# A decoder step on one core: Strassen weight forms made eight K tiles at a time, and 16 K tiles instead of 14 in the heads

## The chip, the cores and the metric

The kernel runs on one core of one Trainium2 chip. The metric is the device time of one execution in microseconds (us); the median of three runs is given. TensorE multiplies, ScalarE (ACT in the profile) and VectorE (DVE) work element by element, GpSimd (POOL) and SyncE (SP) mostly start transfers.

## The reference, cut to what matters

Two layers are computed for 512 prompt tokens and 8 sample tokens, which share all weights. The model width is 2048; everything is float32.

```python
def trunk_layer(x, p_i, pos, conv_buf, ret_S, norm_g, w_in, conv_w, gn_g, w_out, w_pg, w_ple):
    h = rmsnorm(x, norm_g)
    z = h @ w_in                                   # 2048 -> 8192 columns
    b_c, c_c, x_c, g_c, q, k, v, g_r = split_projection(z)
    conv_y, new_buf = short_conv(c_c * x_c, conv_buf, conv_w)
    y_conv = b_c * conv_y * jax.nn.silu(g_c)
    q = rope(q...); k = rope(k...) * (RET_HEAD_DIM ** -0.5)
    o, new_S = retention(q, k, v, ret_S, retention_log_gamma())
    ...                                            # norm over each head
    y_ret = (o * gn_g) * jax.nn.silu(g_r)
    x = x + jnp.concatenate([y_conv, y_ret], axis=-1) @ w_out      # 2048 -> 2048
    x = x + jax.nn.sigmoid(x @ w_pg) * (p_i @ w_ple)               # 2048 -> 2048
    return x, new_buf, new_S
```

A final RMS norm follows. Four large products per layer (w_in, w_out, w_pg, and the small w_ple) hold nearly all the arithmetic.

## The kernel before

**Layout.** Activations lie transposed: 16 K tiles of 128 model columns, each 128 partitions by 520 tokens (512 and 8). The tokens are cut into two halves, LEFT and RIGHT, of 260. A weight column block is 128 columns wide, so a matmul is a 128x128 weight tile times 260 tokens.

**Three matmuls for one.** To keep float32 accuracy each operand is split into a rounded part and a remainder. `split_w` makes the two weight parts: ScalarE copies the raw weights into `hi` (L229), VectorE subtracts to get `lo` (L230). `mm3` then issues `hi*x_hi`, `hi*x_lo` and `lo*x_hi` (lines L247, L248, L249).

**Pairs by Strassen.** Two column blocks are computed together by `pair`. Where its number of rows `s` is not 0, the first `s` K tiles go through `strassen` in the seven-product form: column blocks, even and odd K tiles and token halves form a 2x2 by 2x2 product. Each of the seven products runs over q = s/2 K tiles. `raws` loads the four raw weight forms w11, w21, w22 and w12, `add` combines them in place on VectorE (L319, four times per pair), and `times` splits a form and multiplies it. The K tiles from `s` to 16 are done plainly afterwards. With s = 16 there is nothing left over: the pair then takes three PSUM banks (a, b, d) instead of four, and two of the results go straight into slots.

**Banks and copies.** A bank is copied out while products keep being added to it: for instance bank `a` takes w11·k1, is copied into d, takes w21·t2 (the third product), is copied into z0, takes w11·t3 (the fifth), is read out again, and takes w22·t4. Those copies are line L307, on ScalarE (`copy`) or VectorE (`plus`). The next matmul on the bank waits for its copy.

**Chunks.** `add` and `times` cut the q tiles into chunks of at most CHA and CHS tiles. With 4, seven tiles are cut 3 and 4, eight tiles 4 and 4. `CHL` cuts the loads. Raw forms live in a ring of 32 tiles taken in eights (so four forms), the split parts in a ring of 60 tiles.

**Stages.** For each layer: the heads (16 pairs of w_in for q, k, v and the gate of four retention heads; the first two of layer 0 are done outside `pair`), the convolution (16 pairs of w_in), the mixer output (8 pairs of w_out) and the gate (8 pairs of w_pg, 7 in the last layer). `HEADS`, `CONVS`, `OUT_ROWS` and `GATES` hold `s` for each pair. Retention itself (`steps`), sample states and operand sums are spread between them.

**Order.** The program is written once and a list scheduler, with priorities, decides the order of the instructions on each engine. Every engine then works through its own list in that order; an instruction that waits holds back all behind it on its engine.

Of the kernel before, what the change touches and what calls it, by code (L numbers as in the profile page):

```python
# [28 lines left out]
EPS = 1e-6  # L29
NSLOT = 75  # L30
CH = 4
CHS = 4
CHA = 4
CHL = 4
CK = 256
BUSY = 10**9
# [13 lines left out]
EARLY = 6  # L50


HEADS = [[0, 0, 0, 8] + [14] * 12, [0] + [14] * 15]
CONVS = [[14] * 2 + [16] * 13 + [14]] * 2
OUT_ROWS = [[0, 8, 16, 16, 16, 16, 16, 0]] * 2

MIXED, MIX = 64, [*range(8, 14), *range(8), 14, 15]
# [134 lines left out]
def trunk_kernel(  # L192
# [32 lines left out]
    def split_w(raw, slot=False):  # L225
        n = raw.shape[1]
        hi, lo = (getr()[:, :n] if slot and not split_ring.fits(n // P) else split_ring.get(n // P) for _ in range(2))
        with tc.high_priority(offset=WPRIO):
            S.activation(hi, raw, AF.Copy)  # L229
            V.tensor_tensor(lo, raw, F(hi), SUB)  # L230
        return hi, lo

    def chunks(a, b, most=CH):

        n = (b - a + most - 1) // most
        e = [a + (b - a) * i // n for i in range(n + 1)] if n else [a]
        return list(zip(e, e[1:]))
# [52 lines left out]
    def strassen(x, src0, src1, s, step=None):  # L290
# [24 lines left out]
        def add(out, x, y, op):  # L315
            for i, j in chunks(0, q, CHA):
                n = slice(P * i, P * j)
                with tc.high_priority(offset=WPRIO):
                    V.tensor_tensor(out[:, n], x[:, n], y[:, n], op)  # L319

        def times(out, raw, xs, start, more):
            for i, j in chunks(0, q, CHS):
                w = split_w(raw[:, P * i : P * j])
                product(out, w, 0, xs[i:j], start and i == 0, j == q, more)
                split_ring.put(*w)
# [237 lines left out]
    def norm_g(l, k):  # L563
        return vec[:, 16 * l + k : 16 * l + k + 1]
# [97 lines left out]
    def from_dram(src):  # L662
        def load(k):
            t = get()
            SIDE.dma_start(t, src[k])
            return t

        return load

    xs = []  # L670
    X = Operands(HEADS[0][2:] + CONVS[0], from_dram(xT), gain=lambda k: norm_g(0, k))
    X.todo = [t for t in ((i, False, True) for i in range(max(X.rows) // 2))]
# [43 lines left out]
    for l in range(DEPTH):  # L716
# [456 lines left out]
        if not tail:  # L1173
            X = Operands(HEADS[l + 1] + CONVS[l + 1], next_in, RESERVE_NEXT, gain=lambda k, l=l: norm_g(l + 1, k))
        for m in range(0, KT - tail, 2):
# [303 lines left out]
```

## Time and profile before

| what | value |
|---|---|
| median of three runs (lowest, highest) | 2166.96 us (2166.78, 2170.64) |
| span of the profiled execution | 2167.3 us |
| TensorE (PE) busy | 2147.8 us, 99% |
| VectorE (DVE) busy | 1896.1 us, 87% |
| ScalarE (ACT) busy | 1264.5 us, 58% |
| mean traffic of the transfers | 179 GB/s |

The page gives no other time for the profiled execution than its span, 2167.3 us, which is 0.3 us above the median. The profile gives busy time per engine, groups of equal instructions with their mean length, who waited for whom, and every instruction in order of time. A matmul's listed length (some 0.28 us) is longer than the distance between two matmuls (some 0.12 us), since they overlap in the array; a gap between two matmuls is therefore read from their starts.

By the lines that appear in the trace the heads of layer 0 run to about 505 us, the convolution to about 705 us, the mixer output to about 870 us, the gate to about 1110 us; those of layer 1 end at about 1530, 1785, 1930 and 2110 us.

### The profile page before, as it was taken

How to read it: one execution, taken by the hardware profiler on the slowest of the kernel's cores; microseconds unless marked ns; L12 is line 12 of the kernel's file. 1: busy time of each engine (PE TensorE's matmuls, PEld its weight loads, DVE VectorE, ACT ScalarE, POOL GpSimd, SP SyncE). 2: the span in 40 equal slices, each digit the busy share in tenths (PEclk: the TensorE clock that was granted, in tenths of full speed). 3: DMA queues.
4: the chain of work that ended last, by engine and by line, in shares of the span. 5: the costliest groups of instructions: out<-in, count | busy, mean ns of one | idle time of the engine just before them, and what ended most of it. 6: DMA issues, size and time to landing. Idle time of an engine off the chain costs nothing. (4 is left out here: it accounts for less than half of the span.)

```text
span 2167.3 us, 48178 instructions
## 1 busy us (share of the span) xinstructions
PE 2147.8 (99%) x17861; PEld 2142.1 (99%) x17861; DVE 1896.1 (87%) x3849; ACT 1264.5 (58%) x2647; POOL 430.6 (20%) x746
## 2 busy tenths in 40 slices
PE   9999999999999999999999999999999999999998
PEld 9999999999999999999999999999999999999998
DVE  8889988998999987987997988989999998879884
ACT  8656655565555655655765655565645555456565
POOL 2313222211001211200212222231111022011011
PEclk9999999999999999999999999999999999999999
DMA  8555565545543745645645566664464355566455
GB/s 288 171 175 197 181 217 184 178 157 175 158 129 118 238 156 187 215 154 160 215 144 175 172 213 191 189 209 170 151 182 149 120 158 202 176 207 200 128 164 198
DMA packets 182861, 387.31 MB, mean 179 GB/s; under 512 B 25888, under 2 KB 56352, under 8 KB 182624
## 3 DMA queue, kind: packets, MB, share of 16 engines
q1 hardware_dynamic: 128704, 212.98, 31.6%
q0 software_dynamic: 53056, 169.84, 23.8%
q8 instruction: 140, 2.29, 0.4%
q10 hardware_dynamic: 864, 1.39, 0.2%
q14 instruction: 97, 0.79, 0.1%
HBM read 318.96 MB, written 65.15 MB: 177 GB/s over the span
## 5 line engine op out<-in xcount | busy, mean ns | idle before, releaser
L247 PE MATMUL ps_g<-slot,split 128*128 128x260 f32 x5465 | 1531.6, 284 | 7.2 <-ACT slot L307 2.9
L248 PE MATMUL ps_g<-slot,split 128*128 128x260 f32 x5465 | 1534.3, 282 | 0.3 <-DVE slot L555 0.3
L249 PE MATMUL ps_g<-slot,split 128*128 128x260 f32 x5461 | 1519.9, 283 | 0.5 <-DVE split L230 0.5
L229 ACT ACTIVATE split<-raw 128x512 fp32r<-128x512 f32 (+2 forms) x1347 | 777.3, 596 | 583.1 <-DVE raw L319 213.2
L247 PEld LDWEIGHTS ps_g<-slot,split 128*128 128x128 f32 x5465 | 1024.0, 188 | 10.1 <-ACT slot L307 3.7
L248 PEld LDWEIGHTS ps_g<-slot,split 128*128 128x128 f32 x5465 | 1028.5, 188 | 0.5 <-DVE slot L555 0.5
L249 PEld LDWEIGHTS ps_g<-slot,split 128*128 128x128 f32 x5461 | 1019.8, 188 | 1.0 <-DVE split L230 1.0
L230 DVE TENSOR_TENSOR split<-raw,split 128x512 fp32r<-128x512 f32 (+2 forms) x1346 | 849.2, 652 | 172.5 <-PE ps_g L248 85.4
L319 DVE TENSOR_TENSOR raw<-raw 128x512 f32<-128x512 f32 (+1 forms) x660 | 428.9, 660 | 32.5 <-DMA raw<-wi 23.7
L307 ACT ACTIVATE slot<-ps_g 128x260 f32<-128x260 f32 x336 | 127.4, 381 | 140.6 <-PE ps_g L249 122.7
L551 ACT ACTIVATE slot<-slot 128x520 fp32r<-128x520 f32 (+1 forms) x212 | 109.2, 562 | 46.6 <-DVE slot L414 11.1
L552 DVE TENSOR_TENSOR slot<-slot,slot 128x520 fp32r<-128x520 f32 (+1 forms) x212 | 124.4, 620 | 4.1 <-ACT slot L551 3.9
L781 POOL DMA_DIRECT2D o_rets<-slot x64 | 35.3, 552 | 351.6 <-DVE slot L780 131.7
L307 DVE TENSOR_TENSOR slot<-ps_g,slot 128x260 f32<-128x260 f32 x168 | 70.9, 424 | 6.0 <-PE ps_g L249 3.7
L869 POOL DMA_DIRECT2D slot<-hs x64 | 46.2, 724 | 118.7 <-DVE split L230 42.7
L814 POOL DMA_DIRECT2D hs<-slot x64 | 35.6, 556 | 139.3 <-DVE slot L755 61.3
L780 DVE SCALAR_TENSOR_TENSOR slot<-slot,vs,slot 128x256 f32<-128x256 f32 x128 | 56.1, 481 | 4.5 <-ACT slot L776 4.3
L746 DVE TENSOR_TENSOR slot<-slot,slot 128x520 f32<-128x520 f32 x80 | 55.8, 698 | 4.7 <-DMA o_rets<-slot 3.7
L770 POOL DMA_DIRECT2D slot<-sret x64 | 35.5, 554 | 114.6 <-ACT split L229 37.3
L1058 POOL DMA_DIRECT2D slot<-x1s x76 | 40.8, 538 | 87.6 <-PE ps_g L249 27.2
L1209 POOL DMA_DIRECT2D x2s<-slot x30 | 16.4, 545 | 201.6 <-DVE slot L1204 200.6
L771 POOL DMA_DIRECT2D slot<-kq x64 | 34.9, 547 | 106.0 <-DVE slot L876 22.2
(217 smaller groups left out, 1733.8 us busy)
## 6 DMA issues: line engine op xcount, KB each, us to landing
raw<-wi SPq DMA_DIRECT2D x377, 256.0 KB, 3.9
raw<-wo SPq DMA_DIRECT2D x128, 256.0 KB, 5.4
raw<-wg SPq DMA_DIRECT2D x122, 256.0 KB, 4.1
raw<-wi SPq DMA_DIRECT2D x136, 192.0 KB, 4.0
slot<-x1s POOLq DMA_DIRECT2D x76, 260.0 KB, 5.1
slot<-sret POOLq DMA_DIRECT2D x64, 256.0 KB, 4.0
hs<-slot POOLq DMA_DIRECT2D x64, 256.0 KB, 4.0
slot<-hs POOLq DMA_DIRECT2D x64, 256.0 KB, 5.2
```

The lines of the kernel that those rows point to most:

```text
L229: S.activation(hi, raw, AF.Copy)
L230: V.tensor_tensor(lo, raw, F(hi), SUB)
L247: PE.matmul(out, wh, xh, start=start, stop=False, skip_group_check=more)
L248: PE.matmul(out, wh, xl, start=False, stop=False, skip_group_check=more)
L249: PE.matmul(out, wl, xh, start=False, stop=stop, skip_group_check=more)
L307: fn(*args)
L319: V.tensor_tensor(out[:, n], x[:, n], y[:, n], op)
L551: keep(S.activation(hi, src[:, n], AF.Copy))
L552: V.tensor_tensor(lo, src[:, n], F(hi), SUB)
L746: V.tensor_tensor(out[:, n], v, table[:, n], MUL)
L780: keep(V.scalar_tensor_tensor(st[:, c], k, vs[:, h, e, b : b + 1], st[:, c], MUL, ADD))
L869: SIDE.dma_start(t[:, :512].rearrange("p (m n) -> p m n", m=2), src)
```

## The change

Two constants and two tables. `CHS` and `CHA` go from 4 to 8, so that `times` splits a whole form with one ScalarE and one VectorE instruction, and `add` combines whole forms with one VectorE instruction. The head pairs with 14 rows now have 16; of the convolution pairs the first two of each layer go from 14 to 16, and only the last one keeps 14.

```diff
-CHS = 4
-CHA = 4
+CHS = 8
+CHA = 8
...
-HEADS = [[0, 0, 0, 8] + [14] * 12, [0] + [14] * 15]
-CONVS = [[14] * 2 + [16] * 13 + [14]] * 2
+HEADS = [[0, 0, 0, 8] + [16] * 12, [0] + [16] * 15]
+CONVS = [[16] * 15 + [14]] * 2
```

So 27 head pairs and 4 convolution pairs go from 14 rows to 16. All 84 Strassen pairs are touched by the chunks, except those with 8 rows (three of them), whose four tiles were one chunk already. The counts of instructions change as follows (name, shape: before, now):

| engine, line, shape | before | now |
|---|---|---|
| PE, all matmuls | 17827 | 17734 |
| DVE, all | 3851 | 2898 |
| ACT, all | 2655 | 1995 |
| SP, loads | 886 | 824 |
| DVE L230 `lo`, 128x1024 / x896 / x768 / x512 / x384 / x256 | 0 / 0 / 0 / 1031 / 249 / 66 | 546 / 14 / 7 / 143 / 4 / 4 |
| ACT L229 `hi`, the same shapes | 0 / 0 / 0 / 1032 / 249 / 66 | 546 / 14 / 7 / 143 / 4 / 4 |
| DVE L319 `add`, the same shapes | 0 / 0 / 0 / 520 / 140 / 0 | 312 / 8 / 4 / 12 / 0 / 0 |
| ACT L307 copies from bank to bank | 121 | 90 |

**What the order becomes on TensorE.** The place is a convolution pair of layer 0. A bank's name carries a number, so that equal numbers are the same bank in the same pair; `[waits ...]` names the engine whose semaphore is waited for. Before, bank `a` of the pair is ps_g_7737. Its third product ends here:

```order
L247 MATMUL ps_g_7737<-slot27_152_1588,split_73 128x260
L248 MATMUL ps_g_7737<-slot28_153_1589,split_73 128x260
L249 MATMUL ps_g_7737<-slot27_152_1588,split_73 128x260
L247 MATMUL ps_g_7977<-slot2_3_119,split_73 128x260 [waits Activation_49]
L248 MATMUL ps_g_7977<-slot2_3_119,split_73 128x260
L249 MATMUL ps_g_7738<-slot7_8_168,split_73 128x260 [waits DVE_49]
```

Of the 24 rows that follow, 12 belong to bank b and 12 to the next pair's first product (ps_g_7977). Then the fifth product of the same bank begins, which waits for the copy:

```order
L247 MATMUL ps_g_7977<-slot21_22_332,split_73 128x260
L248 MATMUL ps_g_7977<-slot21_22_332,split_73 128x260
L249 MATMUL ps_g_7977<-slot21_22_332,split_73 128x260
L247 MATMUL ps_g_7737<-slot52_79_777,split_73 128x260 [waits Activation_49]
L248 MATMUL ps_g_7737<-slot53_80_778,split_73 128x260
```

Now, at the same place, bank `a` is ps_g_7205 and bank b ps_g_7206. The end of the third product and the start of the fifth on TensorE:

```order
L247 MATMUL ps_g_7205<-slot30_143_1407,split_73 128x260
L248 MATMUL ps_g_7205<-slot34_144_1408,split_73 128x260
L249 MATMUL ps_g_7205<-slot30_143_1407,split_73 128x260
L247 MATMUL ps_g_7206<-slot7_8_168,split_73 128x260 [waits Activation_49]
L248 MATMUL ps_g_7206<-slot8_9_169,split_73 128x260
L247 MATMUL ps_g_7205<-slot52_79_777,split_73 128x260 [waits Activation_49]
L248 MATMUL ps_g_7205<-slot53_80_778,split_73 128x260
```

The half of bank b's product and the beginning of the next pair, which filled the place, have moved behind: two matmuls are left between the bank's last one and its next one, where 24 were. Counted over the whole program, a matmul that waits for a ScalarE copy (L307) of its own bank stands this many rows behind that bank's last matmul:

| rows behind | 1 | 3 | 4 | 5 | 7 | 8 to 16 | 17 or more |
|---|---|---|---|---|---|---|---|
| before, waits | 0 | 0 | 0 | 1 | 1 | 6 | all others |
| now, waits | 6 | 39 | 3 | 1 | 3 | 12 | all others |

**What it becomes on ScalarE.** The place is the same pair. Before, around the copies of bank a (ps_g_7737):

```order
L307 ACTIVATE slot10_426_7740<-ps_g_7739 128x260 [waits DMASW4_49,PE_49]
L229 ACTIVATE split_73<-raw_72 128x512 [waits DVE_49]
L307 ACTIVATE slot10_426_7740<-ps_g_7737 128x260 [waits PE_49]
L229 ACTIVATE split_73<-raw_72 128x512 [waits DMAHW5_49]
L229 ACTIVATE split_73<-raw_72 128x512 [waits DMAHW4_49]
```

Now (ps_g_7205 is bank a, ps_g_7207 bank d):

```order
L307 ACTIVATE slot49_426_7208<-ps_g_7207 128x260 [waits DMASW4_49,PE_49]
L229 ACTIVATE split_73<-raw_72 128x1024 [waits DVE_49]
L307 ACTIVATE slot49_426_7208<-ps_g_7205 128x260 [waits PE_49]
L229 ACTIVATE split_73<-raw_72 128x1024 [waits DMAHW1_49,DMAHW0_49]
L229 ACTIVATE split_73<-raw_72 128x1024 [waits DMAHW7_49,DMAHW6_49]
```

The copies stand as before; the splits between them cover whole forms. The matmul reads only the rows of the split that it needs, but waits for the whole instruction. A `lo` of 1024 whose chain of waits begins at one of the last 11 matmuls ahead of its user stands at 8 places now (2, 4, 4, 4, 4, 6, 8 and 8 rows ahead), a `hi` at 7 (1, 1, 9, 9, 9, 11 and 11 rows); before, two `lo` (5 and 11 rows) and two `hi` (9 and 10 rows) stood so close. For 140 of the 414 waits for a `lo` of 1024 the chain begins 26 to 28 rows ahead.

## The prediction

> **What bounds the kernel now.** I read the page's busy times first, then the groups by form, the waits of TensorE, the stages as windows, and last the instructions in order of time at places where TensorE stands.
>
> ```profile
> span 2167.3 us, 48178 instructions
> PE 2147.8 (99%) x17861; PEld 2142.1 (99%) x17861; DVE 1896.1 (87%) x3849; ACT 1264.5 (58%) x2647; POOL 430.6 (20%) x746
> ...
> 505.00:705.00 200.00, 200.00 (x1672) 200.00 (x1671) 182.33 (x360) 107.21 (x215) 24.87 (x35) 1.00 0.47 142
> 705.00:870.00 165.00, 161.68 (x1344) 161.05 (x1343) 139.96 (x258) 90.92 (x196) 28.42 (x53) 1.00 0.59 193
> 2100.00:2167.30 67.30, 58.17 (x481) 57.22 (x479) 39.53 (x90) 39.04 (x97) 11.95 (x21) 0.98 0.52 181
> ```
>
> In the stage rows stand the window, the busy time and count of PE, PEld, DVE, ACT and POOL, the granted clock, the share and rate of the transfers. TensorE is the bound. In the convolution of layer 0 (505 to 705 us) it has no idle time, and 1672 matmuls take 200 us: 0.1196 us each at a granted clock of 1.00. VectorE at 87% is the next, but the bound only where TensorE waits for it:
>
> ```profile
> PE ps_g L247 <- ACT slot L307: 2.9, 4, 1.3
> PE ps_g L247 <- ACT ps_g L307: 1.6, 2, 1.2
> PE ps_g L247 <- ACT split L229: 1.5, 2, 1.3
> ...
> PE ps_g L249 <- DVE split L230: 0.5, 1, 0.5
> ```
>
> Columns: total, times, longest. TensorE waits for splits three times in the whole program (2.0 us) and for bank copies six times (4.5 us). So time spared on VectorE or ScalarE is worth almost nothing by itself, and a matmul saved is worth its 0.12 us, unless the new order makes TensorE stand.
>
> **The change part by part.**
>
> *Matmuls.* A pair with 14 rows issues 7·7·3 + 2·4·3 = 171 matmuls, one with 16 rows 7·8·3 = 168. With 27 head and 4 convolution pairs that is 31·3 = 93 fewer: 93·0.1196 = **-11.1 us**, on the path.
>
> *Element work.*
>
> ```profile
> L230 DVE TENSOR_TENSOR split<-raw,split 128x512 fp32r<-128x512 f32 x1031 | 695.0, 690 | 147.8 <-PE ps_g L248 81.2 <-ACT split L229 51.8 <-issue 6.1
> L229 ACT ACTIVATE split<-raw 128x512 fp32r<-128x512 f32 x1032 | 632.3, 626 | 462.3 <-DVE raw L319 188.2 <-PE ps_g L249 166.4 <-PE ps_g L248 45.1
> L319 DVE TENSOR_TENSOR raw<-raw 128x512 f32<-128x512 f32 x520 | 354.1, 688 | 17.6 <-DMA raw<-wi 12.1 <-DMA raw<-wo 2.9
> L230 DVE TENSOR_TENSOR split<-raw,split 128x384 fp32r<-128x384 f32 x249 | 137.1, 555 | 16.2 <-ACT split L229 9.9 <-PE ps_g L248 3.4 <-ACT slot L551 1.9
> L307 ACT ACTIVATE slot<-ps_g 128x260 f32<-128x260 f32 x336 | 127.4, 381 | 140.6 <-PE ps_g L249 122.7 <-DVE osum L784 4.6 <-DVE slot L746 4.3
> L229 ACT ACTIVATE split<-raw 128x384 fp32r<-128x384 f32 x249 | 127.2, 518 | 84.0 <-DVE raw L319 25.0 <-PE ps_g L248 24.2 <-PE ps_g L249 17.9
> ```
>
> No row has 1024 elements. From 384 to 512 `lo` grows by 135 ns and `hi` by 108 ns per 128 elements, so my estimates are 690 + 4·135 = 1230 ns and 626 + 4·108 = 1058 ns. VectorE loses 953 instructions; joining two of 512 saves 2·690 - 1230 = 150 ns where they stand alone, and no less than about 60 ns back to back (two of them take 1.29 us in a row below: the second starts 0.60 us after the first). The 16-row form's three more K tiles of `lo` and four more of `add` per pair eat part of it. VectorE ends between 30 and 120 us less busy, ScalarE about as much. All of it lies beside TensorE: worth **0** by the waits above (at most the 2.0 us).
>
> *What the merging costs: lead.* With chunks of 4 the scheduler could fill TensorE with half products of b and of the next pair. Now a form is ready as a whole or not at all, and at 49 places a bank's next product starts 1 to 5 matmuls behind its last (the table in the section on the change; one place before). The copy lies between. Its price, from two places in the trace:
>
> ```profile
> 602.07 0.28 PE L249 MATMUL ps_g<-slot,split 128*128 128x260 f32 x1
> 602.38 1.29 DVE L230 TENSOR_TENSOR split<-raw,split 128x512 fp32r<-128x512 f32 x2
> 602.39 0.39 ACT L307 ACTIVATE slot<-ps_g 128x260 f32<-128x260 f32 x1 [0.19 <-PE ps_g L249]
> ...
> 1117.69 0.28 PE L249 MATMUL ps_g<-slot,split 128*128 128x260 f32 x1
> 1118.17 0.28 PE L248 MATMUL ps_g<-slot,split 128*128 128x260 f32 x1
> 1118.42 0.37 ACT L307 ACTIVATE ps_g<-ps_g 128x260 f32<-128x260 f32 x1
> 1118.85 0.39 PE L247 MATMUL ps_g<-slot,split 128*128 128x260 f32 x1 [0.40 <-ACT ps_g L307]
> 1119.07 0.28 PE L248 MATMUL ps_g<-slot,split 128*128 128x260 f32 x1
> ```
>
> At 602 us ScalarE was free: the copy starts 0.32 us after the bank's last matmul starts and takes 0.39. At 1118 us the matmul starts 0.06 us after the copy ends. From last matmul to next: 0.32 + 0.39 + 0.06 = 0.77 us, where three rows behind would be 0.36. The matmul after a stand comes 0.22 us later instead of 0.12 (1118.85 to 1119.07): another 0.10. So the loss is 0.77 - 0.12·d + 0.10: 0.75 us at d = 1, 0.51 at 3, 0.39 at 4, 0.27 at 5. Sum: 6·0.75 + 39·0.51 + 3·0.39 + 0.27 = **+25.8 us**. This is the least: at 1118 us (d = 5) ScalarE was inside splits, the copy began 0.73 us after the bank's last matmul, and the loss was 0.66 us instead of 0.27. In the row order of the change ScalarE mostly has nothing ahead of the copy but a split that TensorE has used already, so I take the least. Behind the waiting copy stand two splits of 1024; they are of later products, and TensorE's own standing gives them the time back.
>
> *Late splits.* For the 8 close `lo` the same round trip is 0.32 + 1.23 + 0.06 = 1.61 us: 8·(1.61 + 0.10) less 40 rows at 0.12 is 8.9 us. For the 7 close `hi` it is 0.32 + 1.06 + 0.06 = 1.44: 7·1.54 less 51 rows is 4.7 us. Some share a place with a copy; I take **+10 us** (bounds 4 and 13). The 140 `lo` with 26 to 28 rows have 3.1 to 3.4 us for 1.61: another 1024 ahead of them in VectorE's queue fits (1.23), a second does not. The nearest row, TensorE's 0.5 us for `lo` in all, says nearly none pays; if every one paid half a row of 512, it would be 140·0.3 = 42. I take one in twenty at one more 1024 less the rest, about 0.9 us: **+6 us**, near the row.
>
> *Gone.* Stands that exist now: the close copy at 1118 us (0.66 us) and part of the 2.0 us for splits: **-2 us**. The stands at 705 to 870 us (3.3 us) and after 2100 us (9.1 us) stem from a stage's first operands and the tail, and stay.
>
> *Transfers.* SP issues 62 fewer loads (pieces of 3 and 4 tiles become 4 and 4, the left-over pieces go); the bytes are the same. Both halves must now have landed before an `add` starts; the loads have spare time since VectorE waits 17.6 us for them in all 520 rows of `add`. Costed at 0; if that cover is gone, it shows as `add` waiting for raw<-wi.
>
> Sum: -11.1 + 25.8 + 10 + 6 - 2 = +28.7, on a span 0.3 us above the median: 2167.0 + 28.7 = about **2196 us**, 1.3% slower.
>
> [...]
>
> **The rivals.**
>
> *Faster, 2155 us.* VectorE's relief counts and the close copies don't bite. Then -11.1 and nearly the 2.0 us of split waits are gained. It decides at 13/0.51, about 25 places: if fewer than 25 of the 49 make TensorE stand, and no split is late, the change gains. For it: the order comes from a planner, which put two matmuls there as if they sufficed. Against it: 0.77 us is measured twice over, in parts. [...]
>
> *No change, 2167 us.* Half the places bite and nothing else: -13 + 25·0.51.
>
> *Much slower, 2240 us.* Joined instructions become the cadence: the 140 `lo` each pay 0.3 us (+42 for my +6) and the copies meet ScalarE inside a split of 1.06 us in one case of three (49·0.35/3, some +6). For it: ScalarE's and VectorE's instructions are twice as long and each holds its queue. Against it: both engines have 13% and 42% free and end less busy. [...]
>
> **How the numbers follow.** The likeliest, 2196, holds what is certain in the order and least in price: 0.72 for it and what lies around it (2180, the copies, the saved matmuls and nothing else, to 2225). Much slower: 0.15. No change: 0.05. Faster: 0.08. The range of eight in ten runs from 2176 to 2232: it leaves out the two lower cases (0.13) and the upper end of the highest. About 0.2% (4.3 us) is what a measurement of this kernel can tell from no change: faster 0.08, same 0.05, slower 0.87.
>
> **What would show it.** (1) TensorE's count falls by 93, and the distance in undisturbed stretches stays 0.1196. (2) TensorE's wait for "ACT slot L307" grows from 4 times to over 40; the view shows only the part not covered by a matmul's listed 0.28 us, so 0.77 - 0.24 - 0.28 = 0.25 us for each with d = 3, some 12 us in all. (3) In the convolution (no idle before) the gap comes once in every pair of 168 matmuls. (4) Rows of 128x1024 at about 1.23 and 1.06 us; VectorE's busy share near 82 to 85%. I am wrong if TensorE's waits for L307 stay under ten times, if the matmul's distance itself changes, or if `add` waits for raw<-wi by tens of us.

## The result, and the profile after

The changed kernel takes 2255.68 us (median; 2252.15 to 2261.89) against 2168.47 us of the kernel before in the same runs: a ratio of 1.040, with an interval of 1.037 to 1.042. It is 87 us slower; 29 were forecast. The profiled execution has a span of 2260.1 us, 4.4 us above the median and 92.8 us above the profiled span before.

The page's busy times, TensorE's waits (us in total, times, longest) and three stages as windows (columns as in the prediction):

```profile
span 2260.1 us, 45227 instructions
PE 2185.3 (97%) x17768; PEld 2151.7 (95%) x17768; DVE 1860.6 (82%) x2896; ACT 1173.6 (52%) x1987; POOL 435.4 (19%) x746
```

```profile
PE ps_g L247 <- ACT split L229: 17.3, 17, 4.0
PE ps_g L249 <- DVE split L230: 15.5, 18, 2.3
PE ps_g L247 <- ACT slot L307: 14.0, 31, 2.5
PE ps_g L247 <- ACT ps_g L307: 3.7, 5, 1.7
```

```profile
70.00:505.00 435.00, 416.94 (x3373) 409.66 (x3372) 368.20 (x593) 222.01 (x370) 108.82 (x185) 0.99 0.54 173
505.00:705.00 200.00, 197.91 (x1615) 194.21 (x1613) 172.46 (x248) 95.78 (x148) 21.74 (x38) 1.00 0.46 146
1110.00:1530.00 420.00, 398.41 (x3224) 390.82 (x3223) 352.29 (x564) 220.87 (x372) 104.44 (x176) 0.99 0.54 174
```

The 93 matmuls are gone and VectorE is 36 us less busy. But the waits for `hi` (L229) grew from 1.5 to 17.3 us, for `lo` (L230) from 0.5 to 15.5, and for copies to slots (L307) from 2.9 to 14.0. In 200 us of convolution 1615 matmuls start where 1672 did. The view of waits shows only what a matmul's listed length does not cover. So I also took every matmul that starts over 0.14 us after the one before, counted the time above 0.12 us, and put it down to the producer that it waited for last (us, places):

| waited for last | before | after |
|---|---|---|
| ScalarE copy L307 | 5.9 (11) | 25.0 (48) |
| `hi` L229 (before: 512; after: 1024) | 2.9 (5) | 24.0 (44) |
| `lo` L230 (before: 512; after: 1024) | 0.9 (3) | 20.4 (43) |
| other producers | 6.7 | 24.7 |
| none: the matmul behind a stand, or a slow clock | 12.4 | 37.3 |
| all | 28.8 | 131.4 |

That accounts for the result: 131.4 - 28.8 - 11.1 for the matmuls saved = +91.5, where the spans differ by 92.8.

One of the two longest stands, in order of time (start and length in us; in brackets the idle time before it and its releaser):

```profile
314.04 0.28 PE L249 MATMUL ps_g<-slot,split 128*128 128x260 f32 x1
314.36 1.06 ACT L229 ACTIVATE split<-raw 128x1024 fp32r<-128x1024 f32 x1 [0.42 <-PE ps_g L249]
...
316.97 1.06 ACT L229 ACTIVATE split<-raw 128x1024 fp32r<-128x1024 f32 x1 [1.45 <-DMA raw<-wi]
...
317.93 0.65 ACT L307 ACTIVATE slot<-ps_g 128x260 f32<-128x260 f32 x2
...
318.08 0.39 PE L247 MATMUL ps_g<-slot,split 128*128 128x260 f32 x1 [3.75 <-ACT split L229]
...
319.10 0.42 PE L249 MATMUL ps_g<-slot,split 128*128 128x260 f32 x1
...
319.31 0.42 PE L247 MATMUL ps_g<-slot,split 128*128 128x260 f32 x1
...
319.53 0.42 PE L248 MATMUL ps_g<-slot,split 128*128 128x260 f32 x1
```

A `hi` of 1024 waits 1.45 us for a raw load, and TensorE stands for about 4 us until that `hi` is done; the two bank copies come only behind it in ScalarE's queue. Then comes what I had not thought of: from 318.6 us on the matmuls start about 0.21 us apart instead of 0.12, and each is listed with 0.42 us instead of 0.28. The same place as windows:

```profile
300.00:310.00 10.00, 10.00 (x86) 10.00 (x86) 9.38 (x15) 5.58 (x8) 1.28 (x2) 1.00 0.19 59
316.00:318.60 2.60, 0.50 (x2) 0.30 (x2) 1.18 (x3) 1.63 (x4) 0.72 (x1) 1.00 1.00 359
318.60:322.40 3.80, 3.77 (x18) 3.77 (x19) 0.00 (x0) 2.10 (x5) 0.58 (x1) 0.55 0.93 340
322.40:330.00 7.60, 7.60 (x66) 7.60 (x65) 6.65 (x10) 1.06 (x1) 2.39 (x4) 1.00 0.34 117
```

In the stand the transfers were at a share of 1.00 (359 GB/s). Behind it the granted clock (the column of 1.00, 1.00, 0.55, 1.00) is near one half for 3.4 us; then it is full again.

### The profile page after: what moved, and what is told of

It is laid out like the page before. It is cut to its first block, busy times and chain, and to the rows that moved or that the text cites. A ratio compares the mean times of both kernels' runs of the same rounds, so it can differ in the third digit from the quotient of the medians.

```text
span 2260.1 us, 45227 instructions
## 1 busy us (share of the span) xinstructions
PE 2185.3 (97%) x17768; PEld 2151.7 (95%) x17768; DVE 1860.6 (82%) x2896; ACT 1173.6 (52%) x1987; POOL 435.4 (19%) x746
## 3 DMA queue, kind: packets, MB, share of 16 engines
q0 software_dynamic: 53056, 169.84, 22.6%
## 5 line engine op out<-in xcount | busy, mean ns | idle before, releaser
L247 PE MATMUL ps_g<-slot,split 128*128 128x260 f32 x5434 | 1541.1, 286 | 41.2 <-ACT split L229 17.3
L249 PE MATMUL ps_g<-slot,split 128*128 128x260 f32 x5434 | 1518.6, 285 | 16.9 <-DVE split L230 15.5
L230 DVE TENSOR_TENSOR split<-raw,split 128x1024 fp32r<-128x1024 f32 (+3 forms) x718 | 784.5, 1104 | 290.9 <-ACT split L229 169.1
L229 ACT ACTIVATE split<-raw 128x1024 fp32r<-128x1024 f32 (+3 forms) x718 | 681.6, 960 | 581.0 <-DVE raw L319 318.2
L319 DVE TENSOR_TENSOR raw<-raw 128x1024 f32<-128x1024 f32 (+2 forms) x336 | 401.8, 1196 | 19.8 <-DMA raw<-wg 12.7
L307 ACT ACTIVATE slot<-ps_g 128x260 f32<-128x260 f32 x336 | 127.5, 382 | 245.0 <-PE ps_g L249 232.4
L307 DVE TENSOR_TENSOR slot<-ps_g,slot 128x260 f32<-128x260 f32 x168 | 71.3, 424 | 9.3 <-PE ps_g L249 9.3
L771 POOL DMA_DIRECT2D slot<-kq x64 | 35.2, 550 | 106.4 <-DVE slot L876 33.1
```

The lines of the kernel that those rows point to most:

```text
L247: PE.matmul(out, wh, xh, start=start, stop=False, skip_group_check=more)
L249: PE.matmul(out, wl, xh, start=False, stop=stop, skip_group_check=more)
L307: fn(*args)
```

## The experiments

Ratios are to the kernel before, timed in the same runs.

### The two parts apart

Theory A put the loss into the joined chunks, theory B into the 16 rows. In the first run, rows alone, chunks as before:

```diff
 # changed kernel
-CHS = 8
-CHA = 8
+CHS = 4
+CHA = 4
```

> Chunks of 4 as before, only the rows of the changed kernel (16 in the heads). Theory A (the loss comes from whole-form chunks of 8: a split is ready late and TensorE is left without a half product to fill in): 93 matmuls fewer are worth 11 us and little is lost, 2155 to 2168 us; TensorE's waits for splits stay under 6 us. Theory B (the loss comes from 16 rows in the heads, whose VectorE work per pair is larger while TensorE's time is shorter): 2215 us or more.

Measured: 2186.54 us, 1.0077 (1.0063 to 1.0091). Neither theory: the rows alone are 17 us slower though 11 us of matmuls are gone, so they cost some 28.

The chunks alone:

```diff
 # kernel before
-CHS = 4
-CHA = 4
+CHS = 8
+CHA = 8
```

> Chunks of 8, rows as before (14 in the heads). Theory A: most of the loss is there, 2168 + 60 to 90, so 2228 to 2258 us, with TensorE waiting for splits and copies at some 80 to 130 places. Theory B: under 2190 us.

Measured: 2230.09 us, 1.0285 (1.0271 to 1.0299), as A expected. The joined chunks are the larger part: 61 us, with 18 for the rows 79 of the 87. Of them the adds alone:

```diff
 # kernel before
-CHA = 4
+CHA = 8
```

> Only the add of whole forms (CHA 8), splits in chunks of 4, rows as before. Theory A in the form that the split's chunk decides (it holds the ring and is what TensorE waits for): 2163 to 2175 us. If the longer chain of adds were the cause instead: 2200 us or more, with TensorE waiting for splits behind adds.

Measured: 2192.72 us, 1.0109 (1.0092 to 1.0126): a miss. Joining the adds alone spares VectorE instructions (1880.5 us busy against 1896.1) and still costs 24 us; why, no run shows.

### The split ring

A ring of 60 tiles holds seven runs of 8; with 64 it holds eight.

```diff
 # changed kernel
-SPLIT = 60
+SPLIT = 64
```

> The changed kernel with the ring of split parts at 64 tiles instead of 60: eight places of eight tiles (four products) instead of seven and four tiles that no form of eight can use. Theory A1 (the ring's lead is the cause: with seven places the split of a product waits for a product three or four back, so TensorE runs out): close copies fall from 49 to 6 places in the order, and the time falls to 2175 to 2200 us. Theory A2 (the instructions' own length is the cause: hi then lo of 1024 one after the other, 2.3 us, before a product may start): it stays above 2235 us.

Measured: 2227.02 us, 1.0272 (1.0255 to 1.0289), between the two ranges: 29 us better than the changed kernel, and still 58 us behind the one before. In the order the matmuls that wait for a copy at most five rows behind their bank's last matmul fell from 49 to 6. Yet the copies still made TensorE stand at 34 places, 24.3 us by the count above, and `hi` of 1024 for 20.8. TensorE's waits there:

```profile
PE ps_g L247 <- ACT split L229: 20.1, 11, 4.8
PE ps_g L247 <- ACT slot L307: 12.0, 17, 1.8
PE ps_g L247 <- ACT ps_g L307: 7.2, 7, 1.4
...
PE ps_g L249 <- DVE split L230: 2.2, 4, 0.8
```

The waits for `lo` are gone (15.5 to 2.2). Those for `hi` and for the copies are not. Followed back, no copy's stand comes straight from the bank's last matmul any more (32 places, 12.6 us, in the changed kernel); most of them, 18.4 us at 26 places, have a `hi` ahead of the copy in ScalarE's queue. So something else holds ScalarE.

### The raw ring

Theory R: the raw ring of 32 holds exactly four forms of 8. A `hi` of 1024 needs both halves of its load, and the places come back only after the `lo` of 1024 that reads them too, so the next load starts late.

```diff
 # changed kernel
-RAW = 32
+RAW = 40
-SPLIT = 60
+SPLIT = 56
```

> The changed kernel (2256 us) with a raw ring of 40 tiles in place of 32, and the split ring cut from 60 to 56 to make room; both split rings hold seven runs of 8 tiles. Theory R (a whole form of 8 tiles is freed and loaded as one, and the raw ring holds exactly four, so the hi splits stand waiting for raw<-wi, the copies behind them in ScalarE's queue stand too, and the longest stands drop the clock): the stands rooted in raw<-wi (33 us after) fall under 12 and the half-clock windows with them, 2205 to 2230 us. Rival (the loads are late since they are issued late in the plan, not for lack of a place, or only the order written for close banks counts): 2240 to 2265, raw<-wi still over 25 us.

Measured: 2211.16 us, 1.0196 (1.0179 to 1.0213): 44.5 us off, in R's range, though the split ring is smaller. ScalarE's waits for splits and loads in the changed kernel, then with the larger raw ring, and last its wait for loads in the kernel before:

```profile
ACT split L229 <- DVE raw L319: 318.2, 119, 7.2
ACT slot L307 <- PE ps_g L249: 232.4, 149, 4.7
ACT split L229 <- DMA raw<-wi: 81.4, 54, 3.1
```

```profile
ACT split L229 <- DVE raw L319: 346.7, 99, 7.7
ACT slot L307 <- PE ps_g L249: 222.9, 158, 6.7
ACT split L229 <- PE ps_g L248: 98.5, 60, 5.1
ACT split L229 <- issue: 85.0, 18, 8.3
ACT slot L1199 <- DVE slot L307: 28.4, 10, 3.0
```

```profile
ACT split L229 <- DMA raw<-wi: 75.6, 59, 3.5
```

The wait for raw<-wi, third in the changed kernel with 81.4 us, has fallen below the fifth row's 28.4. But in the kernel before ScalarE waited for loads nearly as long, 75.6 us. So these waits hardly grew; what grew is the time that TensorE stands for them, as the next table shows. Following each of TensorE's stands back through the waits to the event that began the chain (us, places; "TensorE" means a matmul shortly before, by whose end a ring place or a bank came free):

| the chain began at | before | after | raw ring 40 | split ring 64 |
|---|---|---|---|---|
| load raw<-wi | 4.7 (11) | 33.2 (62) | 3.0 (4) | 23.7 (24) |
| TensorE | 1.6 (5) | 33.8 (78) | 31.3 (80) | 13.6 (24) |

The raw ring takes away the stands that began at a load, the split ring most of those that began at TensorE. The mean granted clock is 0.998 with the raw ring of 40, against 0.992. No run has both rings larger, so a sum of the two gains (73 us) is only argued.

### Is it the ring, or merely another order?

Any change of a ring makes the scheduler order the program anew. Three controls on the kernel before, with chunks of 4: the room that the raw ring took, a larger split ring, and the larger raw ring.

```diff
-SPLIT = 60
+SPLIT = 56
```

> The kernel before with the split ring cut from 60 to 56 tiles and nothing else: the price of the room that the larger raw ring takes. With chunks of 4 the ring holds 14 pieces in place of 15: 2167 to 2178 by every theory. Over 2185 and the two runs with 40 raw tiles are read with that price taken off; below 2165 and the order of the kernel before was not the best for its ring.

Measured: 2191.78 us, 1.0107 (1.0092 to 1.0122): with four places less the kernel is 22.6 us slower, more than any theory allowed.

```diff
-SPLIT = 60
+SPLIT = 64
```

> The kernel before with a split ring of 64 tiles in place of 60, nothing else. Theory P (the order before is a tuned one, and any change of a ring that makes the program be ordered anew loses about 20 us, as the ring of 56 did: 2192 us): 2180 to 2200 though the ring is larger. Rival (the 22 us of the ring of 56 were the price of four places, so a larger ring gives some back): 2150 to 2168.

Measured: 2166.51 us, 0.9989 (0.9981 to 0.9997): no loss, so theory P in its strict form (each new order loses 20 us) falls. It is no gain beyond what can be told from no change either. One run without a loss does not show that a new order never loses.

```diff
-RAW = 32
+RAW = 40
-SPLIT = 60
+SPLIT = 56
```

> The kernel before with raw ring 40 and split ring 56, beside 2192 us for split ring 56 alone. With chunks of 4 a raw half is freed after its own split, so a fifth form should matter far less than in the changed kernel, where it took 45 us off: 2178 to 2195. Rival (raw places are as short in chunks of 4): 2145 to 2165, and then a larger raw ring is worth more than either part of the change.

Measured: 2183.22 us, 1.0064 (1.0051 to 1.0077): beside the split ring of 56 alone, eight raw places give 8.6 us back here, against 44.5 in the changed kernel.

The splits alone joined, with the ring that holds eight of them:

```diff
 # kernel before
-CHS = 4
+CHS = 8
-SPLIT = 60
+SPLIT = 64
```

> The kernel before (14 rows, adds in chunks of 4) with only the splits joined to whole forms and a split ring of 64. Theory R with the ring: splits joined cost little once the ring holds their forms and the raw places are not tied up by joined adds: 2168 to 2190. Rival (a whole-form split is itself late, since its first product waits for a pair of 2.3 us in place of 1.2 us): 2200 to 2225, with waits for L229 and L230 of 896 and 1024 over 20 us.

Measured: 2223.13 us, 1.0253 (1.0236 to 1.0270). The time is the rival's, and the waits for `hi` and `lo`, 16.5 and 4.1 us, come to just its 20; but `lo`, the end of the pair that the rival blamed, has little of them.

```profile
PE ps_g L247 <- ACT split L229: 16.5, 18, 3.8
PE ps_g L247 <- ACT slot L307: 7.2, 7, 2.5
...
PE ps_g L249 <- DVE split L230: 4.1, 8, 1.0
```

Followed back, 37 stands (23.9 us) began at raw<-wi: joined splits alone tie the raw ring up, though the adds are still in halves.

### What the 16 rows cost

Theory R and the places in the split ring were tried on the 16 rows too:

```diff
 # 16 rows, chunks of 4
-RAW = 32
+RAW = 40
-SPLIT = 60
+SPLIT = 56
```

> 16 rows in the heads with chunks of 4 as before (2187 us with raw 32 and split 60), now raw ring 40 and split ring 56. Theory R: the rows cost because the four raw forms of a 16-row step fill the raw ring with no plain tile between; with a fifth place the kernel comes to 2160 to 2176, below or at the kernel before. Rival (the rows cost through the longer chain of products without plain tiles as cover, not through raw): 2182 to 2195.

Measured: 2205.57 us, 1.0167 (1.0152 to 1.0182): outside both ranges. 14 rows with the same rings took 2183.22 us, so the rows cost no less than with the old rings, and R does not explain them.

```diff
 # 16 rows, chunks of 4
-SPLIT = 60
+SPLIT = 64
```

> 16 rows in the heads with chunks of 4 (2187 us with a ring of 60), now with a split ring of 64. Rival to P (places decide): 2155 to 2172, perhaps below the kernel before. Theory P (ordered anew, no gain from places): 2180 to 2200.

Measured: 2188.77 us, 1.0098 (1.0083 to 1.0114), in P's range here: split places give nothing back either. With equal rings, 16 rows less 14 rows is +17.6 us (raw 32, split 60), +22.3 (32, 64) and +22.4 (40, 56). So with chunks of 4 the rows cost about 20 us net with each of these rings, and some 31 with the matmuls that they save.

The heads in windows, the kernel before and then the rows alone, whose busy times stand last:

```profile
70.00:505.00 435.00, 434.06 (x3627) 433.81 (x3627) 394.40 (x852) 258.61 (x563) 111.64 (x192) 1.00 0.58 185
...
1110.00:1530.00 420.00, 418.93 (x3495) 417.74 (x3494) 373.86 (x810) 244.19 (x543) 100.91 (x174) 1.00 0.58 183
```

```profile
70.00:505.00 435.00, 425.09 (x3515) 423.09 (x3514) 394.70 (x807) 246.98 (x507) 112.37 (x192) 0.99 0.56 182
...
1110.00:1530.00 420.00, 410.43 (x3367) 407.17 (x3366) 376.80 (x762) 234.84 (x480) 103.51 (x173) 0.99 0.55 177
```

```profile
PE 2148.9 (98%) x17768; PEld 2138.6 (98%) x17768; DVE 1920.7 (88%) x3787; ACT 1256.0 (57%) x2554; POOL 431.8 (20%) x746
```

VectorE (the third busy time) is at 90% in both, 768 and 772 us of 855; TensorE does 240 matmuls less in the same time. Theory V: VectorE sets the pace, and 16 rows give it 24.6 us more work (1920.7 against 1896.1 us busy), three more K tiles of `lo` and four of `add` in each pair. Theory T: the plain tail of two K tiles, gone with 16 rows, was the cover for the banks' drains. VectorE work added to the 14-row kernel:

```diff
 # kernel before, in head(m), behind pair
+V.tensor_tensor(scratch, rb[:, :512], rb[:, :512], ADD)
+V.tensor_tensor(scratch[:, :260], rb[:, :260], rb[:, :260], ADD)
```

> The kernel before (14 rows) with two more VectorE additions for each head pair (128x512 and 128x260, about 0.69 + 0.43 us, some 27 to 30 us in all, which nobody waits for). Theory V (in the heads VectorE, busy 394 us of 435 in both kernels, is what sets the pace, and 16 rows cost since their adds and splits are some 25 us more of it): 2185 to 2205. Rival T (16 rows cost because the plain tail of two K tiles, whose products cover the drains of the banks, is gone; VectorE's other 9% are free): 2165 to 2178.

Measured: 2193.47 us, 1.0107 (1.0090 to 1.0124). The page and the heads:

```profile
PE 2158.3 (98%) x17861; PEld 2147.1 (98%) x17861; DVE 1920.6 (87%) x3909; ACT 1261.4 (57%) x2647; POOL 431.3 (20%) x746
```

```profile
70.00:505.00 435.00, 427.89 (x3545) 424.70 (x3544) 396.19 (x863) 249.63 (x546) 110.93 (x191) 1.00 0.59 182
...
1110.00:1530.00 420.00, 408.67 (x3350) 404.22 (x3349) 371.27 (x815) 233.09 (x522) 102.97 (x172) 0.99 0.56 173
```

VectorE is busy 24.5 us more (the added rows alone list 33.1, but instructions back to back overlap: at 602 us in the kernel before, two `lo` of 0.69 us in a row took 1.29). Nobody waits for these results, yet the kernel is 24.3 us longer, and the heads look like those with 16 rows: 767 us of VectorE and 227 matmuls less. Then work was taken from VectorE, first by moving half of the rope to GpSimd, in the 16-row kernel with chunks of 4 and in the kernel before:

```diff
-V.tensor_tensor(t2, a, rs, MUL)
+G.tensor_tensor(t2, a, rs, MUL)
...
-V.tensor_tensor(b, b, rc, MUL)
-V.tensor_tensor(b, b, t2, ADD)
+G.tensor_tensor(b, b, rc, MUL)
+G.tensor_tensor(b, b, t2, ADD)
```

> 16 rows with chunks of 4 (2187 us) with three of the rope's six 128x520 operations moved from VectorE to GpSimd, which is busy 26% there: 48 x 0.70 = 33 us off VectorE. Theory V: 2150 to 2172. Rival T: 2180 to 2190, no gain, since VectorE is not what is short. Slower than 2195 and GpSimd's operations hold up VectorE, or the retention that follows.

> The kernel before with the same three rope operations on GpSimd. Theory V: the heads' pace rises here too, 2140 to 2160, faster than before. Rival T: 2163 to 2172, the same. Slower than 2175: GpSimd holds others up.

Measured: 2210.66 us, 1.0192 (1.0172 to 1.0212), and 2204.65 us, 1.0164 (1.0148 to 1.0179). Both are slower, and as a test of V both say nothing, since VectorE was not relieved. From the second, the page's busy times and two groups:

```profile
PE 2158.5 (98%) x17861; PEld 2148.0 (97%) x17861; DVE 1915.5 (87%) x3801; ACT 1262.0 (57%) x2647; POOL 514.5 (23%) x794
```

```profile
L756 POOL TENSOR_TENSOR slot<-slot,slot 128x520 f32<-128x520 f32 x16 | 36.4, 2277 | 28.9 <-DVE slot L754 25.1 <-ACT split L229 3.8
...
L230 DVE TENSOR_TENSOR split<-raw,split 128x384 fp32r<-128x384 f32 x249 | 147.4, 594 | 18.8 <-ACT split L229 12.1 <-PE ps_g L248 4.4 <-ACT slot L551 1.8
```

48 operations less, and VectorE is 19 us busier than in the kernel before: its `lo` of 384 take 594 ns instead of 555. The 16 of them that run at the same time as one of the moved operations take 1243 ns on the mean, the other 233 take 550. GpSimd needs 1.4 to 2.3 us for what takes VectorE 0.70. So the move did not help, and VectorE is slowed meanwhile; by what, no run shows. As the next step the same operations were left out altogether (the second half of the rotation is not computed), in both kernels:

```diff
-V.tensor_tensor(t2, a, rs, MUL)
...
-V.tensor_tensor(b, b, rc, MUL)
-V.tensor_tensor(b, b, t2, ADD)
```

> 16 rows with chunks of 4 (2187 us) with the second half of the rotation of queries and keys left out: 48 VectorE operations of 128x520, 48 x 0.70 = 33 us, all in the heads, and nothing put on another engine in their place (on GpSimd they took 2.28 us each and made VectorE's own longer, so that VectorE was relieved of nothing). Theory V: VectorE's time falls from 1921 to about 1888 and the kernel to 2150 to 2165. Rival T, or an order that loses whatever it has to do: 2178 to 2195.

> The kernel before with the same operations left out, as the control: VectorE from 1896 to about 1863. Theory V in its strong form (VectorE sets the pace of the 14-row heads as well): 2135 to 2150. Weak form (with 14 rows TensorE is at its own limit, 99% busy, and VectorE just keeps up): 2160 to 2170, so that the rows alone push the heads over to VectorE. Rival T: 2160 to 2172 here, and no gain in the 16-row kernel.

Measured: with 16 rows 2167.73 us, 1.0005 (0.9995 to 1.0015), and with 14 rows 2168.02 us, 0.9999 (0.9989 to 1.0008). The page's busy times, 16 rows first:

```profile
PE 2141.0 (99%) x17768; PEld 2134.4 (98%) x17768; DVE 1894.8 (87%) x3739; ACT 1258.6 (58%) x2554; POOL 433.0 (20%) x746
```

```profile
PE 2146.6 (99%) x17861; PEld 2141.3 (99%) x17861; DVE 1871.1 (86%) x3801; ACT 1268.3 (59%) x2647; POOL 429.6 (20%) x746
```

VectorE's busy time falls by 26 us (from 1920.7) and by 25 (from 1896.1). That takes 19 us off the 16-row kernel (to just outside V's 2150 to 2165) and nothing off the 14-row one: nearest to V in its weak form. With 14 rows VectorE just keeps up, and the run that added work paid for it in full. T, which expected no gain with 16 rows, is out as the main cause, but the 16-row kernel should now be 11 us ahead and is level: about 11 us of the rows' cost stay unexplained. Nor does a loss of some 20 us point to VectorE by itself: the split ring of 56 and the joined adds lost 23 and 24 us with no more VectorE work (1897.1 and 1880.5 us busy). How much a new order has to do with each of these losses is not shown.

## Why the prediction missed

The direction was right, and so was the price of a close copy; the size was not. The step that failed is the pricing of late splits at +16 us and of transfers at nothing. In their place the waits for splits rose by 40.6 us, and 33.2 us of TensorE's stands began at a weight load, 4.7 before. Copies (+19.1), splits (+40.6), other producers (+18.0) and stands with no producer (+24.9) make +102.6, less 11.1 for the matmuls. Of the last two the sum held only the 0.10 us for the matmul behind a stand. At 2255.7 us the time lies above even the highest rival, and none of the three signs of being wrong came: the waits for L307 were 31, the spacing in undisturbed stretches was unchanged, and `add` hardly waited for loads.

- *Matmuls, -11.1.* Right: the count fell by 93, and undisturbed stretches run as before (84 start in the 10 us from 300 us, 0.119 apart). By itself, though, the rows' part of the change is a loss.
- *Element work, worth 0.* VectorE did end 36 us less busy, at 82%. But the term covered two opposite things. The joins spare VectorE work; the 16 rows add 24.6 us of it in stages where it stands at 90%. I took 87%, a mean over the span, and TensorE's 0.5 us of waits for `lo` as room; in the run with added work 24.5 us more cost 24.3. In the changed kernel the heads have VectorE at 84%, and the rows still add some 25 us there (2255.7 less 2230.1), so how much of this cause is left is not shown. Another may be the split ring of 60, which has room for eight forms of 7 tiles (14 rows) but for seven of 8.
- *Close copies, +25.8.* The price was right: where the copy follows straight on its bank's last matmul, TensorE stands 0.64 us where it is one row behind (5 places) and 0.37 us three rows behind (24 places); the working gives 0.65 and 0.41 without the 0.10 for the matmul after. That is 12.6 us at 32 places in place of 49. The total came near by luck: the stands behind copies grew by 19.1 us (25.0 less 5.9), but half of the 25.0 are copies late for other reasons. TensorE's wait for L307 to slots rose from 4 to 31 times, under the 40 I named, and from 2.9 to 14.0 us, where I had said some 12. In the convolution the 57 matmuls missing in 200 us are 6.8 us, in ten pairs or so 0.7 us a pair, more than one gap of 0.51. The run with the split ring of 64 shows that nearness in the order was only one way to be late: with 6 close places left, copies still cost 24.3 us, mostly behind a `hi` in ScalarE's queue. Only 4.4 us of that began at a weight load, 6.9 at a matmul.
- *Late splits, +10 and +6.* The first term that failed. It measured 44.4 us (24.0 for `hi`, 20.4 for `lo` of 1024), less 3.8 before. I priced a chain only where it began within the last rows ahead of its user, and each alone. Followed back, 23.3 us of these stands began at raw<-wi and about 15 at a matmul that had to free a place. With a fifth raw place the first kind is nearly gone, with an eighth split place the second falls to 6.5; I weighed neither ring.
- *Transfers, 0.* The second term that failed. I looked for the lost cover at `add`, where it does not show (raw<-wi before `add` fell from 23.7 to 5.1 us); nor does it show in ScalarE's own wait for loads (75.6 and 81.4 us). It shows where TensorE stands: 33.2 us began at raw<-wi, 13.3 of it through `hi`, 9.9 through `lo` and 4.0 through copies. A fifth raw place took 44.5 us off. The 23.3 us of splits among it are counted under both terms.
- *The half clock.* Not in the sum at all. After stands of 1.4 to 4.2 us the granted clock is 0.5 for 3.4 us: nine such windows in eight places, 30.7 us, ahead of the last 6 us of the span, where the kernel before has none. From 18 matmuls in 3.8 us instead of some 32, one window loses about 1.6 us, nine of them some 15 us, an estimate. No run isolates it.
- *The rivals.* "Much slower, 2240" was nearest, but mostly for another reason: less that longer instructions hold a queue (7.9 us of copies stood behind a `hi`) than that the rings hold too few of them.

Open is also what remains when both ring gains are taken off: 2255.7 - 44.5 - 28.7 = 2182.5 if they add, 14 us above the kernel before and 25 above the one with only the matmuls saved. No version tried beats the kernel before by more than its measurement can tell; with the split ring of 64 it is level.

## What to carry to other kernels

Before joining instructions, count how many joined pieces each ring holds: a ring that held eight halves loosely holds four wholes exactly. A wait that cost next to nothing before (here 4.7 us of stands that began at a weight load) then makes the bound engine stand (33.2 us), both for the joined instruction and for what is queued behind it. Read an engine's load in the stage where the work is added, not over the span: at 90% and with hardly any waits for it to be seen, 25 us more on VectorE made the kernel 24 us longer, and taking 25 us away gave nothing back. When a ring or a chunk is changed, run the kernel before with the same ring as a control, since a split ring of four places less moved this one by 23 us.

## What was unexpected of the hardware

The granted clock falls to one half for 3.413 us (once 6.8 us) after some stands of TensorE, and not the longest stands alone are followed by it: in the kernel before with a split ring of 56 such a window begins 1.0 us after the start of a matmul that came 1.6 us late, while in the changed kernel stands of about 1.8 us passed without one.

So where a stand falls counts, and not its length alone. Within a run these windows lie on one grid of 3.413 us. Cut along that grid, from 8 us to the tail, the changed kernel's trace has eight full-speed windows with a half-speed one behind them; 3 to 12 matmuls start in each, where some 28 fit, and every other full-speed window holds at least 14. With the split ring of 56 it is 2 to 10 (five windows) against 15 and more; the kernel before, where none falls ahead of the tail, has none under 15. Over the traces of all 18 kernels the 42 windows with up to 10 all had half speed behind them, and of those from 14 up only two had (15 and 17 matmuls); from 11 to 13 it went both ways. So here few matmuls in one such window went with the half clock behind it, and none of the eight windows of the changed kernel stood wholly idle.

The other surprise is GpSimd's effect on VectorE above: 48 operations moved away, and VectorE 19 us busier.
